# A two-layer decoder trunk on one core: TensorE's part of gates and routing issued later, routing ahead of gates, 95 instead of 78 first products ahead

## The chip, the cores and the metric

The kernel runs on one core of a Trainium2 chip. The metric is the device time of one execution in microseconds (us); lower is better.

## The reference, cut to what matters

512 tokens of width 1024 go through two layers. Each layer has a token mixer and then a product-key expert mixer (`peer`), both with a residual. The change touches the expert mixer alone.

```python
q = (t @ w_q).reshape(n_tok, 8, 2, 64)
scores = jnp.einsum('thpk,hpnk->thpn', q, sub_keys)
s_top, i_top = lax.top_k(scores, 16)
cand = s_top[:, :, 0, :, None] + s_top[:, :, 1, None, :]
...
best, pos = lax.top_k(cand, 16)
expert = jnp.take_along_axis(cand_idx, pos, axis=-1)
gates = jax.nn.softmax(best, axis=-1)
...
u = u_emb[eb]
act = jax.nn.gelu(jnp.einsum('td,thkd->thk', tb, u)) * gb
out = jnp.einsum('thk,thkd->td', act, v_emb[eb])
```

Each token picks 16 of 16384 experts in each of 8 heads, 128 in all. An expert is a row of `u` and a row of `v`.

## The kernel before, in words

The 512 tokens are four tiles of 128. Tile 0 (`GT`) takes its experts by gathers: rows of `u` and `v` come by indirect DMA (`gather`), VectorE multiplies and sums the `u` rows (`products`, tile `junk`), TensorE sums the `v` rows (`sums`, tile `av`), and VectorE adds them to the residual `x`. The gathers run beside the rest, a few at a time (`take`), and `EARLY` says how many are taken before the blocks begin.

Tiles 1 to 3 (`DT`, 384 tokens) go through all 16384 experts as dense products, in 128 blocks of 128 experts. `up(b)` is the first product of block b: 24 matmuls of 384 columns into `pu`, whose activation goes to `H`. The 32-bit weights are split into two bfloat16 halves, so that every product is three matmuls (`mm3`): ScalarE makes `whi` (L71), GpSimd or VectorE `wlo` (L72). `block(b)` multiplies `H` by the gates `G` of that block and makes the second products into six accumulators `acc`.

The gates are dense too: expert by token. They are made in a stage ahead of the blocks, tile by tile. `routing(i)` scores the keys (TensorE, tile `ps`, whose key matrix comes by a DMA on ScalarE's queue), finds the sixteen best on VectorE, and ends with three transposes on TensorE into `pt` (L748 to L750), which ScalarE copies to `i1T`, `i2T` and `ghl`. `gate_group(n)` then serves 16 tokens: VectorE makes four masks (`o2`, `ol`, `oh`, L921 to L926), TensorE multiplies them token by token into `pg`, four tokens in a bank (L932, L933), ScalarE evacuates these into `st` (L934), and a DMA on its queue writes 1 MB to `Gd` in memory (L935). A tile has eight such groups. `oh` and `st` have one buffer each.

Between these steps stand the fillers. The stage is cut into units: one for each step of a routing, three for each gate group, `UNITS` = 183. `fill(n)` counts n units and at each issues its share of the early gathers and of the first products. The products of blocks 0 to `RUN[1]` - 1 = 77 are made so, ahead of the blocks; those of blocks below `SPILL` = 60 are written to `Hd` and read back by `again` two blocks before use, and the other 18 (`AHEAD`) stay in the ring `H`. In the blocks, `block(b)` makes the further first products, one for each block from 60 on, and `tick` takes gathers. A scheduler orders the instructions of each engine by priority within what the data allow, so an engine's order can differ somewhat from the code's.

The order of the stage, before:

```python
            for i in DT:
                for _ in routing(i):
                    fill(1)
                for n in range(NG // ND):
                    gate_group(DT.index(i) * (NG // ND) + n)
                    fill(3)
```

Of the kernel before, what the change touches and what calls it, by code (L numbers as in the profile page):

```python
# [14 lines left out]
F32 = mybir.dt.float32  # L15
BF = mybir.dt.bfloat16
I32 = mybir.dt.int32
U32 = mybir.dt.uint32
AF = mybir.ActivationFunctionType
# [18 lines left out]
DT = [1, 2, 3]  # L38
# [5 lines left out]
KEYS = 128  # L44

KB = 8
GB = 16
NG = TD // GB

SPILL = 60  # L50
AHEAD = 18
LEAD = 6
PACE = 1
OUT1 = 6
RUN = [0] + [min(KEYS, AHEAD + max(b, SPILL)) for b in range(KEYS)]
SLACK = 12
# [1 line left out]
PARTS = 4  # L58

UNITS = ND * 37 + 3 * NG  # L60
EARLY = 80
SHARE = 8
END = 2

# [10 lines left out]
def mm3(nc, out, pairs, start=True, stop=True):  # L75
    n = len(pairs)
    for i, ((ah, al), (bh, bl)) in enumerate(pairs):
        nc.tensor.matmul(out, ah, bh, start=start and i == 0, stop=False)  # L78
        nc.tensor.matmul(out, ah, bl, start=False, stop=False)  # L79
        nc.tensor.matmul(out, al, bh, start=False, stop=stop and i == n - 1)  # L80


class Stream:
# [20 lines left out]
    def next(self, a):  # L104
        while len(self.ready) < self.ahead and self.drams:
            self.emit()
        return tuple(p.rearrange("p (a b) -> p a b", a=a) for p in self.ready.pop(0))
# [420 lines left out]
def layer(tc, nc, k, A, l):  # L528
    ut, vt = A["u"][l], A["v"][l]
    with ExitStack() as es:  # L530
        dram = es.enter_context(tc.tile_pool(name=f"dram{l}", bufs=1, space=bass.MemoryType.DRAM))
        Gd = dram.tile([KEYS // KB, 128, NG, KB * GB], F32, name="Gd")
        Hd = dram.tile([SPILL, 128, TD], F32, name="Hd")
        left = ExitStack()
# [101 lines left out]
        def routing(i):  # L636
# [30 lines left out]
            for a in list(range(8)) + [8]:  # L667
                if a < 8:
                    n = CAND[a]
                    s1, s2 = top[:, :, 0, a:a + 1].to_broadcast([128, HEADS, n]), top[:, :, 1, :n]  # L670
                    i1, i2 = tf[:, :, 0, a:a + 1].to_broadcast([128, HEADS, n]), tf[:, :, 1, :n]
                else:
                    n = 8
# [18 lines left out]
            for a in range(5):  # L692
                n = CAND8[a] if a < 4 else 4
# [7 lines left out]
            for j0, h0, nh in ((0, 0, 4), (0, 4, 4), (8, 0, 2), (8, 2, 2), (8, 4, 2), (8, 6, 2)):  # L701
                n = NCAND if j0 else NC8
# [41 lines left out]
            e2 = rt.tile([128, 2, NS], F32, tag="e2", name="e2", bufs=1)  # L744
            nc.vector.tensor_copy(e2, ei)
            ts = slice(i * 128 - D0, (i + 1) * 128 - D0)
            pt = pr.tile([128, 4, 128], F32, tag="r", name="pt")
            nc.tensor.transpose(pt[:, 0], e2[:, 1], k.ident)  # L748
            nc.tensor.transpose(pt[:, 1], e2[:, 0], k.ident)
# [13 lines left out]
        with ExitStack() as e2:  # L763
# [3 lines left out]
            ahead = pre.enter_context(tc.tile_pool(name=f"ps_a{l}", bufs=2, space=PSUM, reuse_waits="tile"))  # L767
            first = late.enter_context(tc.tile_pool(name=f"first{l}", bufs=2, side="right", reuse_waits="tile"))
# [112 lines left out]
            def take(n):  # L881
                flush()
                for _ in itertools.islice(steps, n):
                    taken[0] += 1
# [9 lines left out]
            def up(b):  # L894
                w = k.W.next(KD)
                p = (psum if b >= RUN[1] or b % 3 == 0 else ahead).tile([128, 512], F32, tag="u", name="pu")[:, :TD]
                mm3(nc, p, [((w[0][:, q], w[1][:, q]), (hhi[:, q], hlo[:, q])) for q in range(KD)])
                if b < SPILL:
                    h = work.tile([128, TD], F32, tag="Hs", name="Hs", bufs=3)
                else:  # L900
                    h = H[b] = work.tile([128, TD], F32, tag="H", name="H", bufs=AHEAD + 1)
                nc.scalar.activation(h, p, AF.Gelu_apprx_tanh)  # L902
                if b < SPILL:
                    nc.scalar.dma_start(Hd[b], h)

            def again(b):
                if b < SPILL:
                    H[b] = work.tile([128, TD], F32, tag="Hs", name="Hs", bufs=3)
                    nc.sync.dma_start(H[b], Hd[b])

            def gate_group(n):

                ts = slice(n * GB, (n + 1) * GB)
                shape = [128, GB // 2, KEYS, 2]

                def by_token(x):
                    return x[:, ts].rearrange("p (a b) -> p a b", b=2)[:, :, None].to_broadcast(shape)

                keys = iot[:, None].to_broadcast(shape)
                o2 = first.tile(shape, BF, tag="o2", name="o2")  # L920
                nc.vector.tensor_tensor(o2, keys, by_token(i2T), op=OP.is_equal)  # L921
                ol = first.tile(shape, BF, tag="ol", name="ol")
                nc.vector.tensor_tensor(ol, keys, by_token(i1T), op=OP.is_equal)
                oh = first.tile(shape, BF, tag="oh", name="oh", bufs=1)
                nc.vector.tensor_tensor(oh, ol, by_token(ghl[:, 0]), op=OP.mult)
                nc.vector.tensor_tensor(ol, ol, by_token(ghl[:, 1]), op=OP.mult)  # L926
                st = first.tile([128, KEYS, GB], F32, tag="st", name="st", bufs=1)
                for c in range(0, GB, 4):
                    pv = ahead.tile([128, 4, KEYS], F32, tag="g", name="pg", bufs=3)
                    for t in range(4):  # L930
                        a, j = divmod(c + t, 2)
                        nc.tensor.matmul(pv[:, t], o2[:, a, :, j], oh[:, a, :, j], start=True, stop=False)  # L932
                        nc.tensor.matmul(pv[:, t], o2[:, a, :, j], ol[:, a, :, j], start=False, stop=True)  # L933
                    nc.scalar.activation(st[:, :, c:c + 4], pv.rearrange("p t k -> p k t"), AF.Copy)  # L934
                nc.scalar.dma_start(Gd[:, :, n].rearrange("p e x -> e p x"),  # L935
                                    st.rearrange("e (p k) t -> e p (k t)", k=KB))

            units, ups = [0], iter(range(RUN[1]))

            def share_of(n):  # L940
                return units[0] * n // UNITS - (units[0] - 1) * n // UNITS

            def fill(n):
                for _ in range(n):
                    units[0] += 1
                    take(share_of(EARLY))
                    for j in itertools.islice(ups, share_of(RUN[1])):
                        up(j)

            for i in DT:  # L950
                for _ in routing(i):
                    fill(1)
                for n in range(NG // ND):
                    gate_group(DT.index(i) * (NG // ND) + n)
                    fill(3)
            for j in ups:
                up(j)
            flush()
# [61 lines left out]
def program(tc, A, out):  # L1020
    nc = tc.nc
    k = Ctx()
    with ExitStack() as es:
        const = es.enter_context(tc.tile_pool(name="const", bufs=1, reuse_waits="tile"))
        k.small = es.enter_context(tc.tile_pool(name="small", bufs=2, reuse_waits="tile"))
        k.W = Stream(nc, es.enter_context(tc.tile_pool(name="wst", bufs=1, reuse_waits="tile")))
        k.ident = const.tile([128, 128], F32, name="ident")
        make_identity(nc, k.ident)
        k.eps = const.tile([128, 1], F32, name="eps")
        nc.vector.memset(k.eps, EPS)  # L1030
        k.junk = const.tile([128, D], BF, name="junk")
        k.x, k.order = [], list(range(NT))
        for i in range(NT):
            x = const.tile([128, D], F32, name=f"x{i}")
            nc.sync.dma_start(x, A["x"][i * 128:(i + 1) * 128, :])
            k.x.append(x)
        for l in range(2):
            layer(tc, nc, k, A, l)
        last = es.enter_context(tc.tile_pool(name="last", bufs=2, side="right", reuse_waits="tile"))
        g = last.tile([128, D], F32, tag="gain", name="gain", bufs=1)  # L1040
        nc.sync.dma_start(g, A["final_norm"].to_broadcast([128, D]))
        for i in k.order:
            h = last.tile([128, D], F32, tag="hrow", name="hrow", bufs=4)
            norm_rows(nc, k, i, g, h)
            nc.sync.dma_start(out[i * 128:(i + 1) * 128, :], h)
# [95 lines left out]
```

## Time and profile before

| what | value |
|---|---|
| median of 3 runs | 3656.72 us (3650.55 to 3668.97) |
| the profiled execution | 3656.95 us, its span 3655.1 us |
| mean granted TensorE clock | 0.961 |
| TensorE busy | 3238.0 us (89%) |
| VectorE, ScalarE, GpSimd busy | 2333.4, 1445.0, 1899.5 us |

The span is the time from the first to the last instruction. Busy time is the time in which at least one instruction of the engine was at work. The page of the profile names groups of instructions by line, engine and tile; the windows give the busy time of each engine in a stretch; the waits say what an idle engine was released by. PE is TensorE, DVE VectorE, ACT ScalarE, POOL GpSimd, and SP the engine whose queue issues most loads.

### The profile page before, as it was taken

To read this page: it belongs to the slowest core of one execution; us is meant where nothing else is said; L and a number is where in the kernel's file an instruction comes from. 1 tells how busy PE (TensorE), PEld (TensorE's weight loads), DVE (VectorE), ACT (ScalarE), POOL (GpSimd) and SP (SyncE) were. 2 spreads that over 40 slices of the span, in tenths; PEclk is the share of its full clock that TensorE was granted. 3 is DMA by queue.
4 is the path that set the end of the run, shared out by engine and by line. 5 is a ranking of instruction groups with operands and counts; after the bars stand their busy time and mean duration, and the time that the engine had idled before them with its cause. 6 is when DMAs were issued, how large, how long until landed. Compare 5 with 4: busy or idle time off the path is not lost. (4 is left out here: it accounts for less than half of the span.)

```text
span 3655.1 us, 52111 instructions
## 1 busy us (share of the span) xinstructions
PE 3238.0 (89%) x19558; PEld 1737.9 (48%) x19786; DVE 2333.4 (64%) x4302; ACT 1445.0 (40%) x2303; POOL 1899.5 (52%) x1106
## 2 busy tenths in 40 slices
PE   8999977877879999999988888778787799999999
PEld 4444554544434444444455555445454344444443
DVE  6554388787756656643567774796868566656534
ACT  5454433333333333333445565333333333333333
POOL 4445755555546566655233345554555356666552
PEclk9999988989989999999999999989998899999999
DMA  4223656877789987886322124568786899878773
GB/s 147 81 89 109 188 171 225 267 225 240 235 306 351 349 300 269 280 292 237 119 77 63 59 71 153 160 216 260 240 268 195 295 345 354 314 283 285 277 264 127
DMA packets 326844, 803.00 MB, mean 220 GB/s; under 512 B 26816, under 2 KB 165568, under 8 KB 322496
## 3 DMA queue, kind: packets, MB, share of 16 engines
q1 hardware_dynamic: 126720, 446.78, 36.6%
q0 software_dynamic: 73728, 268.47, 20.6%
q10 hardware_dynamic: 126144, 84.43, 7.3%
q8 instruction: 155, 2.54, 0.3%
q14 instruction: 97, 0.79, 0.1%
HBM read 723.54 MB, written 76.02 MB: 219 GB/s over the span
## 5 line engine op out<-in xcount | busy, mean ns | idle before, releaser
L72 POOL TENSOR_TENSOR wlo<-w,whi 128x1024 bf16<-128x1024 f32 x520 | 1178.9, 2269 | 1363.7 <-ACT whi L71 1325.8
L71 ACT ACTIVATE whi<-w 128x1024 bf16<-128x1024 f32 x696 | 730.3, 1051 | 769.4 <-PE pu L79 387.5
L78 PE MATMUL pu<-hh,whi 128*128 128x384 bf16 x2048 | 686.1, 335 | 18.2 <-ACT Hs L902 18.2
L79 PE MATMUL pu<-hl,whi 128*128 128x384 bf16 x2048 | 685.2, 335 | 0.0
L80 PE MATMUL pu<-hh,wlo 128*128 128x384 bf16 x2048 | 684.7, 334 | 0.0
L79 PE MATMUL acc<-wlo,ah 128*128 128x512 bf16 x1492 | 567.3, 380 | 34.5 <-ACT ah L71 27.5
L80 PE MATMUL acc<-whi,al 128*128 128x512 bf16 x1492 | 567.2, 380 | 2.3
L78 PE MATMUL acc<-whi,ah 128*128 128x512 bf16 x1470 | 558.9, 380 | 2.3
L807 DVE CUSTOM_DVE_ANT_0 junk<-g,hr 128x1024 bf16<-128x1024 f32 x256 | 360.7, 1409 | 88.2 <-DMA g<-u_in,ix 74.3
L78 PEld LDWEIGHTS <-whi 128*128 128x128 bf16 x2944 | 293.0, 100 | 246.6 <-issue 67.4
L72 DVE TENSOR_TENSOR al<-a,ah 128x384 bf16<-128x384 f32 x256 | 151.5, 592 | 400.8 <-ACT ah L71 400.4
L79 PEld LDWEIGHTS <-whi 128*128 128x128 bf16 x2944 | 293.1, 100 | 217.6 <-issue 40.5
L778 POOL DMA_INDIRECT g<-v_in,ix x256 | 322.3, 1259 | 139.6 <-PE av L832 85.5
L71 ACT ACTIVATE ah<-a 128x384 bf16<-128x384 f32 x256 | 133.6, 522 | 648.5 <-issue 482.3
L80 PEld LDWEIGHTS <-wlo 128*128 128x128 bf16 x2944 | 293.3, 100 | 197.8 <-issue 19.6
L778 POOL DMA_INDIRECT g<-u_in,ix x256 | 307.8, 1202 | 110.6 <-issue 33.7
L72 DVE TENSOR_TENSOR wlo<-w,whi 128x1024 bf16<-128x1024 f32 x176 | 215.0, 1222 | 210.0 <-ACT whi L71 210.0
L78 PEld LDWEIGHTS <-ah 128*128 128x128 bf16 x1536 | 150.4, 98 | 258.6 <-ACT ah L71 54.1
L80 PEld LDWEIGHTS <-al 128*128 128x128 bf16 x1536 | 150.5, 98 | 182.4 <-issue 1.4
L79 PEld LDWEIGHTS <-ah 128*128 128x128 bf16 x1536 | 150.6, 98 | 172.2 <-issue 5.1
L932 PE MATMUL pg<-oh,o 128*128 128x128 bf16 x768 | 108.8, 227 | 111.7 <-ACT st L934 62.8
L79 PE MATMUL mm<-hlo,whi 128*128 128x512 bf16 x500 | 191.1, 382 | 1.4 <-DVE hlo L72 0.5
(384 smaller groups left out, 4942.3 us busy)
## 6 DMA issues: line engine op xcount, KB each, us to landing
w<-ut_in SPq DMA_DIRECT2D x256, 512.0 KB, 4.0
w<-v_in SPq DMA_DIRECT2D x256, 512.0 KB, 5.2
Gd<-st ACTq DMA_DIRECT2D x48, 1024.0 KB, 6.9
G<-Gd SPq DMA_DIRECT2D x32, 1536.0 KB, 8.3
w<-w_in SPq DMA_DIRECT2D x88, 512.0 KB, 3.6
w<-wo_in SPq DMA_DIRECT2D x64, 512.0 KB, 3.7
Hd<-Hs ACTq DMA_DIRECT2D x120, 192.0 KB, 5.3
Hs<-Hd SPq DMA_DIRECT2D x120, 192.0 KB, 6.3
```

What stands on the lines that cost most here:

```text
L71: nc.scalar.activation(hi, src, AF.Copy)
L72: return (lo_eng or nc.vector).tensor_tensor(lo, src, hi, op=OP.subtract)
L78: nc.tensor.matmul(out, ah, bh, start=start and i == 0, stop=False)
L79: nc.tensor.matmul(out, ah, bl, start=False, stop=False)
L80: nc.tensor.matmul(out, al, bh, start=False, stop=stop and i == n - 1)
L778: nc.gpsimd.indirect_dma_start(out=g, out_offset=None, in_=tab, in_offset=bass.IndirectOffsetOnAxis(ap=ix, axis=0))
L807: nc.vector.tensor_tensor_reduce(k.junk, g, hr, op0=OP.mult, op1=OP.add, scale=1.0, scalar=0.0, accum_out=h[:, s:s + 1])
L932: nc.tensor.matmul(pv[:, t], o2[:, a, :, j], oh[:, a, :, j], start=True, stop=False)
```

## The change

The constants change: `SPILL` from 60 to 84, `AHEAD` from 18 to 11, so that `RUN[1]` goes from 78 to 95; `EARLY` from 80 to 100. `routing` yields `True` ahead of its transposes, and `route` puts that last part, and `gate_group` its matmuls, evacuations and write (`multiply`), into a list `due` that `fill` empties three units later. `oh` and `st` get a second buffer. The tiles' routings and gates are issued in the order routing 1, routing 2, gates 1, routing 3, gates 2, gates 3. The shares of the first products are counted for 89 (`REST` = 6 fewer), and what is left is issued after the last group.

```diff
-SPILL = 60
-AHEAD = 18
+SPILL = 84
+AHEAD = 11
...
-EARLY = 80
+EARLY = 100
+
+REST = 6
...
             nc.vector.tensor_copy(e2, ei)
             ts = slice(i * 128 - D0, (i + 1) * 128 - D0)
+            yield True
             pt = pr.tile([128, 4, 128], F32, tag="r", name="pt")
             nc.tensor.transpose(pt[:, 0], e2[:, 1], k.ident)
...
-                oh = first.tile(shape, BF, tag="oh", name="oh", bufs=1)
+                oh = first.tile(shape, BF, tag="oh", name="oh")
                 nc.vector.tensor_tensor(oh, ol, by_token(ghl[:, 0]), op=OP.mult)
                 nc.vector.tensor_tensor(ol, ol, by_token(ghl[:, 1]), op=OP.mult)
-                st = first.tile([128, KEYS, GB], F32, tag="st", name="st", bufs=1)
-                for c in range(0, GB, 4):
...
-                    nc.scalar.activation(st[:, :, c:c + 4], pv.rearrange("p t k -> p k t"), AF.Copy)
-                nc.scalar.dma_start(Gd[:, :, n].rearrange("p e x -> e p x"),
-                                    st.rearrange("e (p k) t -> e p (k t)", k=KB))
-
-            units, ups = [0], iter(range(RUN[1]))
+
+                def multiply():
+                    st = first.tile([128, KEYS, GB], F32, tag="st", name="st")
+                    for c in range(0, GB, 4):
...
+                        nc.scalar.activation(st[:, :, c:c + 4], pv.rearrange("p t k -> p k t"), AF.Copy)
+                    nc.scalar.dma_start(Gd[:, :, n].rearrange("p e x -> e p x"),
+                                        st.rearrange("e (p k) t -> e p (k t)", k=KB))
+
+                due.append((units[0] + 3, multiply))
+
+            units, ups, due = [0], iter(range(RUN[1])), []
...
-                    for j in itertools.islice(ups, share_of(RUN[1])):
+                    for j in itertools.islice(ups, share_of(RUN[1] - REST)):
                         up(j)
-
-            for i in DT:
-                for _ in routing(i):
-                    fill(1)
+                    while due and due[0][0] <= units[0]:
+                        due.pop(0)[1]()
+
+            def route(i):
+                st = routing(i)
+                for last in st:
+                    if last:
+                        due.append((units[0] + 3, lambda: next(st, None)))
+                    else:
+                        fill(1)
+                    if last:
+                        return
+
+            def gate(i):
                 for n in range(NG // ND):
                     gate_group(DT.index(i) * (NG // ND) + n)
                     fill(3)
+
+
+            for i in DT:
+                route(i)
+                if i != DT[0]:
+                    gate(i - 1)
+            gate(DT[-1])
+            while due:
+                due.pop(0)[1]()
             for j in ups:
                 up(j)
             flush()
```

How the instructions move is seen at three places. The line numbers of the changed kernel are two to five higher.

The first is ScalarE at the end of the first routing of layer 0. `sc<-ps` is the evacuation of a head's scores, of the next routing here; `i1T`, `i2T` and `ghl` come from the transposes; `st` is the first gate group. Before, and then with the change:

```order
L71 ACTIVATE whi<-w_5460 128x1024
L902 ACTIVATE Hs<-pu 128x384
L751 ACTIVATE i1T<-pt 128x128
L904 DMA Hd<-Hs 128x384
L752 ACTIVATE i2T<-pt 128x128
L71 ACTIVATE ghl<-pt 128x128
L71 ACTIVATE whi<-w_5546 128x1024
...
L934 ACTIVATE st<-pg 128x128x4 x4
```

```order
L905 ACTIVATE Hs<-pu 128x384
L655 ACTIVATE sc<-ps 128x256
L907 DMA Hd<-Hs 128x384
L651 DMA key<-keys_in 128x256
L73 ACTIVATE whi<-w_5539 128x1024
...
L754 ACTIVATE i1T<-pt 128x128
L755 ACTIVATE i2T<-pt 128x128
L73 ACTIVATE ghl<-pt 128x128
L651 DMA key<-keys_in 128x256
```

The copies of the transposes now come after the first heads of the next routing, and no gate group follows them.

The second is VectorE where the first masks of tile 1 are made (`o`, `ol`, `oh`). Before, they stand behind the end of the same tile's routing; with the change, among the maxima of the next tile's:

```order
L745 CAST e_5312<-ei 128x256
L807 ISA junk,hk<-g,hr 128x1024
...
L921 TENSOR_TENSOR o_5322<-iot,i2T 128x2048
L72 TENSOR_TENSOR ghl<-pt,ghl 128x128
L923 TENSOR_TENSOR ol<-iot,i1T 128x2048
L921 TENSOR_TENSOR o_5408<-iot,i2T 128x2048
L925 TENSOR_TENSOR oh<-ol,ghl 128x2048
```

```order
L661 MATCH_REPLACE sc_5585<-wk,sc 128x128
L663 MAX_INDEX ui<-wk,sc_5579 128x8
L662 MAX wk<-sc_5585 128x8
L924 TENSOR_TENSOR o_6355<-iot,i2T 128x2048
L663 MAX_INDEX ui<-wk,sc_5585 128x8
L926 TENSOR_TENSOR ol<-iot,i1T 128x2048
L659 MAX wk<-sc 128x8 x2
```

The third is ScalarE at the end of the stage; `ah<-a` is the input of the first block. Before, and then with the change:

```order
L902 ACTIVATE H<-pu 128x384
L71 ACTIVATE whi<-w_9461 128x1024
L934 ACTIVATE st<-pg 128x128x4 x4
L935 DMA Gd<-st 128x16x128
L71 ACTIVATE ah<-a_9418 128x384
```

```order
L939 ACTIVATE st<-pg 128x128x4 x4
L940 DMA Gd<-st 128x16x128
L905 ACTIVATE H<-pu 128x384
L73 ACTIVATE whi<-w_9950 128x1024
L73 ACTIVATE whi<-w_9983 128x1024
L905 ACTIVATE H<-pu 128x384
L73 ACTIVATE whi<-w_10016 128x1024
L905 ACTIVATE H<-pu 128x384
L73 ACTIVATE ah<-a_10076 128x384
```

First products and weight splits now stand between the last write of gates and the first block.

## Rows read from the trace of the kernel before

**Rows 1.** The page: the span, and busy us (share) xinstructions of each engine.

```profile
span 3655.1 us, 52111 instructions
...
PE 3238.0 (89%) x19558; PEld 1737.9 (48%) x19786; DVE 2333.4 (64%) x4302; ACT 1445.0 (40%) x2303; POOL 1899.5 (52%) x1106
```

**Rows 2.** Windows by stage; stretch, length, busy us of PE, PEld, DVE, ACT, POOL, clock, DMA.

```profile
517.00:1042.00 525.00, 403.77 (x2775) 240.66 (x2775) 396.23 (x908) 179.47 (x296) 276.14 (x156) 0.90 0.74 239
2369.00:2890.00 521.00, 401.77 (x2765) 239.92 (x2764) 395.05 (x903) 179.16 (x293) 274.45 (x156) 0.91 0.75 240
1042.00:1797.00 755.00, 746.38 (x3876) 345.63 (x3952) 429.94 (x552) 265.98 (x367) 419.82 (x264) 1.00 0.81 288
2890.00:3647.00 757.00, 750.48 (x3898) 347.65 (x3974) 428.60 (x554) 264.98 (x368) 417.69 (x262) 1.00 0.80 284
```

**Rows 3.** Waits of PE, 517 to 1043 us: us in total, times, longest.

```profile
PE pg L932 <- ACT st L934: 29.9, 13, 4.4
PE pg L932 <- DVE oh L925: 26.3, 8, 12.2
PE acc L79 <- ACT ah L71: 13.8, 1, 13.8
PE pt L748 <- DVE e L745: 13.4, 1, 13.4
PE av L832 <- DVE x L836: 10.5, 2, 8.8
PE pu L78 <- ACT Hs L902: 9.6, 2, 6.5
PE ps L651 <- DMA key<-keys_in: 9.6, 4, 5.9
```

**Rows 4.** Waits of ACT and DVE in the same stage.

```profile
ACT st L934 <- DMA Gd<-st: 63.6, 19, 8.4
...
DVE oh L925 <- PE pg L932: 49.1, 15, 6.4
```

**Rows 5.** Windows of the tile pu alone: busy us of PE and of ACT, clock, DMA.

```profile
537.00:568.00 31.00, 30.40 (x186) 2.36 (x5) 1.00 0.77 252
517.00:1042.00 525.00, 332.53 (x1822) 37.17 (x77) 0.90 0.74 239
```

**Rows 6.** Window of the tile av alone in the first layer's blocks: PE, PEld, DVE.

```profile
1042.00:1797.00 755.00, 55.40 (x416) 8.18 (x416) 35.34 (x52) 1.00 0.81 288
```

**Rows 7.** Windows, columns as in rows 2: 50 us of the stage, the first blocks.

```profile
850.00:900.00 50.00, 39.04 (x223) 22.09 (x219) 36.76 (x201) 15.45 (x26) 28.58 (x19) 0.93 0.85 285
1042.00:1300.00 258.00, 254.24 (x1204) 108.68 (x1228) 172.56 (x237) 91.11 (x124) 148.44 (x96) 0.99 0.92 343
```

**Rows 8.** The page's costliest groups, the products of gathered rows: busy us, mean ns.

```profile
L807 DVE CUSTOM_DVE_ANT_0 junk<-g,hr 128x1024 bf16<-128x1024 f32 x256 | 360.7, 1409 | 88.2 <-DMA g<-u_in,ix 74.3
```

**Rows 9.** The page's DMA issues: count, KB each, us to landing.

```profile
w<-ut_in SPq DMA_DIRECT2D x256, 512.0 KB, 4.0
...
Gd<-st ACTq DMA_DIRECT2D x48, 1024.0 KB, 6.9
G<-Gd SPq DMA_DIRECT2D x32, 1536.0 KB, 8.3
```

**Rows 10.** Timeline of PE around the first routing's end: start us, us, what, idle before.

```profile
598.10 0.47 PE L748 MATMUL pt<-ident,e 128*128 128x128 f32 x1 [13.41 <-DVE e L745]
...
598.79 0.53 PE L78 MATMUL pu<-hh,whi 128*128 128x384 bf16 x1
599.11 0.53 PE L79 MATMUL pu<-hl,whi 128*128 128x384 bf16 x1
```

**Rows 11.** Timeline of DVE and of POOL, 568 to 576 us.

```profile
568.34 0.56 DVE L707 TENSOR_TENSOR eq<-cpos,pf 128x800 bf16<-128x800 bf16 x1
...
572.58 2.50 DVE L707 TENSOR_TENSOR eq<-cpos,pf 128x800 bf16<-128x800 bf16 x1
...
572.52 2.12 POOL L72 TENSOR_TENSOR wlo<-w,whi 128x1024 bf16<-128x1024 f32 x1 [7.52 <-ACT whi L71]
```

More of the change, by code (lines that the diff above doesn't have):

```diff
@@ L923, in gate_group @@
                 nc.vector.tensor_tensor(ol, keys, by_token(i1T), op=OP.is_equal)
-                oh = first.tile(shape, BF, tag="oh", name="oh", bufs=1)
+                oh = first.tile(shape, BF, tag="oh", name="oh")
                 nc.vector.tensor_tensor(oh, ol, by_token(ghl[:, 0]), op=OP.mult)
                 nc.vector.tensor_tensor(ol, ol, by_token(ghl[:, 1]), op=OP.mult)
-                st = first.tile([128, KEYS, GB], F32, tag="st", name="st", bufs=1)
-                for c in range(0, GB, 4):
[L929 to L933, printed above, removed]
-                    nc.scalar.activation(st[:, :, c:c + 4], pv.rearrange("p t k -> p k t"), AF.Copy)
-                nc.scalar.dma_start(Gd[:, :, n].rearrange("p e x -> e p x"),
-                                    st.rearrange("e (p k) t -> e p (k t)", k=KB))
-            units, ups = [0], iter(range(RUN[1]))
+                def multiply():
+                    st = first.tile([128, KEYS, GB], F32, tag="st", name="st")
+                    for c in range(0, GB, 4):
+                        pv = ahead.tile([128, 4, KEYS], F32, tag="g", name="pg", bufs=3)
+                        for t in range(4):
+                            a, j = divmod(c + t, 2)
+                            nc.tensor.matmul(pv[:, t], o2[:, a, :, j], oh[:, a, :, j], start=True, stop=False)
+                            nc.tensor.matmul(pv[:, t], o2[:, a, :, j], ol[:, a, :, j], start=False, stop=True)
+                        nc.scalar.activation(st[:, :, c:c + 4], pv.rearrange("p t k -> p k t"), AF.Copy)
[3 more added lines that the diff above has]
+            units, ups, due = [0], iter(range(RUN[1])), []
             def share_of(n):
```

## The prediction, made before the changed kernel was run

> **What bounds the kernel now.** I read the page first for the share of each engine, then the windows by stage, then the waits of the slow stage, then single stretches of the timeline. One execution spans 3655.1 us and TensorE is busy for 3238.0 of them [rows 1]; no other engine comes near. The windows then show two kinds of stage, each found once per layer [rows 2]. The blocks (757 us and 755 us) are TensorE from end to end: 746.4 of 755 us busy at a granted clock of 1.00. There a product that is taken away shortens the run by its own length. The stage ahead of them, which routes three token tiles and makes their gates, takes 525 and 521 us, and TensorE works for 403.8 of 525 at a mean clock of 0.90. It is idle for 121 us while VectorE is busy for 396.2, the DMA for 0.74 of the time, and nobody is full. So this stage is bound by engines that wait for each other in turn, and it has room for work if those waits can be filled.
>
> The waits of TensorE name the turns [rows 3]: 29.9 us for ScalarE to empty a bank of gates (st), 26.3 for VectorE's masks (oh), 13.8 for the first block's input, 13.4 for the end of a routing (pt), 10.5 for a residual sum, 9.6 for an evacuation, 9.6 for a key's load. Behind the first of these stands a DMA: ScalarE waits 63.6 us for the write of the only st buffer, and whatever else it should split or evacuate waits in line. VectorE in turn waits 49.1 us for TensorE to give back the only oh [rows 4].
>
> **The change part by part, for one layer.**
>
> *17 first products move (78 to 95).* In 537 to 568 us 186 matmuls of first products take 30.40 us at full clock, 163 ns each [rows 5]; a product has 24, so 3.92 us, and 17 have 66.7 us. In the blocks this is saved whole, because TensorE idles for 9 of 755 us there [rows 2]. EARLY also takes 20 gathers ahead. The order of instructions shows 60 instead of 48 second-product matmuls (av) ahead of the first block, three halves of four; 416 records in the blocks are 52 halves for 55.40 us [rows 6], 1.07 us each, 3.2 us in all. Blocks: **-70 us**. The gating stage has the same 70 us of TensorE work more.
>
> What else these products issue: each has a weight load of 512 KB, a ScalarE split and evacuation, and a GpSimd split. 24 more of them (SPILL 60 to 84) are written to memory and read back in the blocks, on the queues of ScalarE and SP. I cost the blocks' reads at nothing. The first blocks already run with such reads at a DMA share of 0.92, and TensorE is busy for 254.2 of 258 us beside it [rows 7]; the change makes that stretch longer (84 blocks instead of 60), not denser, because by the code's counts the gathers per tick stay the same: some 181 over 166 ticks, now some 160 over 149. The 258 us hold the first sixty-odd blocks, so 84 are about 350 us; if the cover went, each per cent by which the transfers fell behind would cost 3.5 us a layer.
>
> *The stage's waits.* The end of a routing (pt) is issued three units later, with the next tile's routing ahead of it. Units carry 0.49 products each (89 over 183, 0.43 before), so about 1.5 products, 6 us, are put ahead of the wait, and three more come from the denser filling. VectorE needs some 6 us more up to there itself (three products at 1.41 [rows 8], and stretched operations, below). I keep 6 of 13.4. For the masks the order shows the first two groups of a tile made inside the next tile's routing, and oh has a second buffer: I keep 5 of 26.3. With two st buffers ScalarE no longer stands still for the write. What is left for TensorE is a split of some 1 us in front of an evacuation: I keep 11 of 29.9. With more products queued TensorE gets to the evacuations later, while VectorE's part of the routing is as long: 3 of 9.6. Before the first block stand four products after the last gates, 15.7 us, against a write of 6.9 and a read of 8.3 us [rows 9] and the block's own first operations. That would cover nearly all of it, but the SP queue now has only two second weights ahead of the three gate reads, where it had seven. The third block's weight queues behind 4.5 MB of gates, so I keep 7 of 13.8. This is what is late next. The residual sum (10.5) and the key loads (9.6) are not touched, and of the remaining 8 us I keep 5. The 121 us become 57: **-64 us**.
>
> *The clock.* [...] In the whole stage 1822 records of first products take 332.53 us instead of 298 (1822 by 163 ns) [rows 5]; a part of these 35 us is only the ends of interrupted runs. [...]
>
> *VectorE and GpSimd.* GpSimd splits 17 more weights, and a compare beside such a split takes 2.50 us instead of 0.56 [rows 11]: 1.9 us for each that is hit, between nothing and 33 us. Nine products more come to 13 us. VectorE then works 409 to 442 us, under the 515 forecast, so I add nothing. ScalarE (179 us of 525) and GpSimd (276) have room for their part [rows 2].
>
> *The sum.* Stage: 525 + 70 - 64 - 16 = 515. Blocks: 755 - 70 = 685. A layer gives back 80 us, and the two are alike within 4 us in all four windows [rows 2], so 160 us. The profiled execution took 3656.95 us, 1.9 more than its span and 0.2 more than the median of the three runs, so no correction is made: **3497 us**.
>
> **The rivals.**
>
> *A: transfers set the stage.* It moved 525 us at 239 GB/s, 125.5 MB [rows 2]. The change adds 17 weights, 20 gathers of the same size and 24 products of 0.2 MB, 24.1 MB, together 149.6. The densest 50 us that I found in the stage reach 285 GB/s [rows 7]; at that rate the stage needs 525 us and gives nothing, 140 us remain: 3517 us. For it: the masks' writes, 1 MB a group, are now bunched behind the last routing. Against it: the blocks hold 343 GB/s [rows 7], by which the stage needs 436. Chance 0.20.
>
> *B: the waits only change place.* VectorE is at work for 396 of 525 us [rows 2], and if its own order sets the stage, TensorE's 70 us come on top: saved and spent cancel, 3657 us, no change. Against it: 49 us of VectorE's idling are waits for the oh that is now doubled [rows 4]. Chance 0.04.
>
> *C: slower, through the clock.* [...] Chance 0.03. [...]
>
> *D: better.* [...] Chance 0.08.
>
> That the change does not do what it says is excluded by the order of instructions: 95 products stand ahead of the first block.
>
> **How the numbers follow.** The forecast has 0.65. Its own spread comes from what I kept of the waits: 30 us of waits and 10 lost to the clock give -111 us a layer (3435), 78 and 22 give -51 (3555). 3435 to 3555 takes in A as well and leaves out B, C and D, 0.15 together, and a little of the forecast's own edges. About half a per cent, 18 us, is what a measurement of this kernel can tell from no change: faster by more is forecast, A and D, 0.93; the same is B, 0.04; slower is C, 0.03.
>
> **What would show it.** In the profile after: blocks of about 685 us at clock 1.00 with TensorE still idle for some 1%; a stage of 500 to 530 us with TensorE about 89% busy (458 of 515) and a clock of about 0.95; no wait of st for the write of Gd and none of oh for TensorE; four products between the last gates and the first block. The forecast is wrong if the blocks show new waits for weights or read-back products, if the stage grows by more than 20 us, or if TensorE waits at pt and st as long as now. A stage near 525 us with a DMA share above 0.9 would be A.

## The result and the profile after

The changed kernel takes 3533.28 us (median of 4 runs, 3529.10 to 3548.67), the kernel before 3653.64 beside it: a ratio of 0.9673, 95% interval 0.963 to 0.9715. The forecast was 3497 us and a gain of 160; 120 came.

The page and the windows by stage of the changed kernel; the columns are those of [rows 2]. As there, the first layer's window of the blocks ends at the first of their residual sums; the table further below runs to the last one and has some 6 us more.

```profile
span 3527.3 us, 52345 instructions
...
PE 3201.8 (91%) x19574; PEld 1728.5 (49%) x19786; DVE 2307.3 (65%) x4286; ACT 1444.2 (41%) x2303; POOL 1931.2 (55%) x1122
```

```profile
515.00:1044.40 529.40, 454.67 (x3186) 275.48 (x3185) 436.55 (x914) 201.40 (x326) 348.21 (x189) 0.93 0.84 280
2299.00:2833.20 534.20, 455.21 (x3190) 275.64 (x3188) 431.25 (x918) 201.37 (x326) 347.71 (x190) 0.93 0.83 278
1044.40:1726.30 681.90, 675.23 (x3457) 305.12 (x3523) 375.42 (x522) 242.97 (x333) 361.79 (x237) 1.00 0.83 298
2833.20:3520.50 687.30, 680.57 (x3479) 307.23 (x3544) 379.57 (x526) 242.24 (x335) 358.57 (x235) 1.00 0.82 293
```

Against [rows 2] the blocks fell from 755 and 757 us to 682 and 687, with TensorE still idle for 1% of them. The gating stage, forecast to fall from 525 to 515, grew to 529 and 534. The waits of TensorE in it, against [rows 3]:

```profile
PE av L835 <- DVE x L839: 29.3, 7, 15.5
PE pu L80 <- ACT Hs L905: 23.8, 2, 13.8
PE pg L938 <- DVE ol L929: 5.7, 5, 1.9
PE ps L653 <- DVE ghl L74: 4.6, 1, 4.6
PE pg L937 <- DVE oh L928: 3.9, 1, 3.9
PE pg L937 <- ACT st L939: 3.7, 7, 2.5
...
PE pt L751 <- DVE e L747: 0.4, 1, 0.4
```

The four waits at which the change aims have nearly gone: st 29.9 to 3.7, oh 26.3 to 3.9, pt 13.4 to 0.4, the first block 13.8 to none. Two others took over: the residual sum 10.5 to 29.3, the evacuation of a first product 9.6 to 23.8. The first comes from VectorE directly. The second comes from it through ScalarE, whose timeline (start, us, what, idle before) shows it standing 17.16 us for a subtraction on VectorE before it goes on to the split and the evacuation:

```profile
580.46 0.31 ACT L720 ACTIVATE wk<-wk 128x128 f32<-128x128 f32 x1 [17.16 <-DVE wk L719]
...
580.91 1.06 ACT L73 ACTIVATE whi<-w 128x1024 bf16<-128x1024 f32 x1
581.99 1.28 ACT L905 ACT_TABLE_LOAD   x1
583.28 0.49 ACT L905 ACTIVATE Hs<-pu 128x384 f32<-128x384 f32 x1
```

The longest wait for a residual sum, 15.54 us, has another side. `av` has one buffer, so TensorE cannot make the next half before VectorE has added the last one to `x`. Below stand the half made before, the sum that it waits for, and the half made after it:

```profile
833.50 1.06 PE L835 MATMUL av<-g,z 128*32 128x512 f32 x8
850.29 0.68 DVE L839 TENSOR_TENSOR x<-x,av 128x512 f32<-128x512 f32 x1
851.03 1.94 PE L835 MATMUL av<-g,z 128*32 128x512 f32 x8 [15.54 <-DVE x L839]
```

In between VectorE worked through the compares of a routing's end. So not only how much VectorE has to do may set such a wait, but also behind what the sum stands in its order. No run here changes that order, or the number of `av` buffers, alone.

The windows of single stretches (columns as before) show how VectorE's load lies: the second routing and the last gates.

```profile
600.00:702.00 102.00, 84.84 (x488) 48.25 (x486) 100.17 (x295) 32.70 (x53) 72.76 (x41) 0.90 0.75 253
...
960.00:1044.00 84.00, 78.36 (x649) 50.83 (x647) 57.65 (x41) 38.36 (x65) 54.65 (x27) 1.00 0.99 342
```

In the second routing VectorE is busy for 100.2 of 102 us; in the last gates for 57.7 of 84, while the DMA stands at 0.99; but TensorE is busy there for 78.4 of 84 us, so at most 5.6 us of the stage are lost in that stretch. Three causes were open for the stage: VectorE (V below), ScalarE's standing (H), or the transfers (D).

### The profile page after: what moved, and what is told of

It is laid out like the page before. It is cut to its first block, busy times and chain, and to the rows that moved or that the text cites. A ratio compares the mean times of both kernels' runs of the same rounds, so it can differ in the third digit from the quotient of the medians.

```text
span 3527.3 us, 52345 instructions
## 1 busy us (share of the span) xinstructions
PE 3201.8 (91%) x19574; PEld 1728.5 (49%) x19786; DVE 2307.3 (65%) x4286; ACT 1444.2 (41%) x2303; POOL 1931.2 (55%) x1122
## 5 line engine op out<-in xcount | busy, mean ns | idle before, releaser
L74 POOL TENSOR_TENSOR wlo<-w,whi 128x1024 bf16<-128x1024 f32 x536 | 1201.9, 2244 | 1223.1 <-ACT whi L73 1136.9
L81 PE MATMUL pu<-hl,whi 128*128 128x384 bf16 x2048 | 677.9, 331 | 0.0
L82 PE MATMUL pu<-hh,wlo 128*128 128x384 bf16 x2048 | 677.2, 331 | 0.2
L810 DVE CUSTOM_DVE_ANT_0 junk<-g,hr 128x1024 bf16<-128x1024 f32 x256 | 382.0, 1492 | 100.7 <-DMA g<-u_in,ix 93.6
L781 POOL DMA_INDIRECT g<-u_in,ix x256 | 321.7, 1257 | 106.3 <-issue 34.5
L74 DVE TENSOR_TENSOR wlo<-w,whi 128x1024 bf16<-128x1024 f32 x160 | 196.3, 1227 | 19.6 <-ACT whi L73 19.2
L835 PE MATMUL av<-g,z 128*32 128x512 f32 x1024 | 141.6, 626 | 65.4 <-DVE x L839 65.4
L1008 DVE TENSOR_TENSOR a<-Hs,G 128x384 f32<-128x384 f32 x168 | 159.2, 948 | 58.6 <-DMA G<-Gd 47.0
```

The lines of the kernel that those rows point to most:

```text
L74: return (lo_eng or nc.vector).tensor_tensor(lo, src, hi, op=OP.subtract)
L781: nc.gpsimd.indirect_dma_start(out=g, out_offset=None, in_=tab, in_offset=bass.IndirectOffsetOnAxis(ap=ix, axis=0))
L810: nc.vector.tensor_tensor_reduce(k.junk, g, hr, op0=OP.mult, op1=OP.add, scale=1.0, scalar=0.0, accum_out=h[:, s:s + 1])
L835: m = nc.tensor.matmul(av[32 * j:32 * j + 32, :], z[:, j, a * 32:a * 32 + 32], rows[j][:, c * 512:(c + 1) * 512], start=True, stop=True)
L1008: nc.vector.tensor_tensor(a.rearrange("p (a b) -> p a b", b=GB), H[b].rearrange("p (a b) -> p a b", b=GB), g, op=OP.mult)
```

## The experiments

The table gives for each run its first products and early gathers ahead of the blocks, the stage (from 15 us after tile 0's indices are made to the first second product) and the blocks (from there to the last residual sum), each for layer 0 and layer 1 of the profiled execution, the median and, with its interval, the ratio to the kernel before as it ran beside each (medians of 3653.64 to 3658.74 us).

| run | products, EARLY | stage, us | blocks, us | run, us | ratio |
|---|---|---|---|---|---|
| before | 78, 80 | 525, 521 | 761, 758 | 3653.64 | 1 |
| the change | 95, 100 | 530, 535 | 688, 687 | 3533.28 | 0.9673 (0.963 to 0.9715) |
| e1_order_only | 78, 80 | 465, 466 | 761, 760 | 3548.17 | 0.9718 (0.9685 to 0.9751) |
| e2_count_only | 95, 100 | 588, 593 | 683, 682 | 3647.07 | 0.9987 (0.9966 to 1.0009) |
| e3_early80 | 95, 80 | 507, 503 | 702, 700 | 3505.81 | 0.9605 (0.9572 to 0.9637) |
| e4_exp_early | 95, 100 | 534, 522 | 688, 690 | 3529.27 | 0.9663 (0.9631 to 0.9696) |
| e5_half_products | 95, 100 | 504, 503 | 689, 688 | 3472.41 | 0.9496 (0.948 to 0.9511) |
| e6_half_rows | 95, 100 | 500, 505 | 690, 687 | 3474.82 | 0.9511 (0.9495 to 0.9527) |
| e7_tile_order | 95, 100 | 541, 539 | 689, 689 | 3557.28 | 0.9736 (0.9719 to 0.9752) |
| e8_one_st | 95, 100 | 574, 578 | 689, 691 | 3621.57 | 0.9902 (0.9886 to 0.9919) |
| e9_early60 | 95, 60 | 473, 475 | 725, 730 | 3486.13 | 0.9524 (0.9495 to 0.9552) |
| e10_rows_in_gates | 95, 80 | 523, 519 | 704, 701 | 3544.23 | 0.9687 (0.9658 to 0.9717) |
| e11_even_transfers | 95, 72 | 499, 491 | 699, 698 | 3482.15 | 0.9529 (0.9515 to 0.9543) |

### e1_order_only and e2_count_only: the two halves of the change

```diff
# e1, against the change
-SPILL = 84
+SPILL = 67
-EARLY = 100
+EARLY = 80
# e2, against the kernel before
-SPILL = 60
-AHEAD = 18
-EARLY = 80
+SPILL = 84
+AHEAD = 11
+EARLY = 100
```

e1 has 78 products as before, of which 67 instead of 60 are written to memory.

> The change with 78 first products and 80 early gathers as before (SPILL 67, AHEAD 11, EARLY 80): the order and the second buffers alone. Three theories of where the 15 to 20 us a layer went that the changed stage took beyond the forecast. V: in a routing VectorE's own queue is full, and TensorE is held at the places where it needs VectorE. H: ScalarE's in-order queue, standing for an exponential or a gelu that VectorE is not ready for, holds TensorE; VectorE itself has room. D: transfers, late gathers above all. By the forecast's own sum (waits and clock give 80 us a layer, whatever is added) the stage is 445 us and the run 3497. V and D: the routings stay VectorE's length, 485 to 500 us a stage, 3585 to 3610. H: 470 us, 3550.

> The kernel before with SPILL 84, AHEAD 11, EARLY 100 alone: 95 products in the old order with single buffers of oh and st. If the added products fill nothing of the waits (rival B of the prediction), the stage is 595 us and the run 3655. If they fill the waits at a routing's end and at the masks, where VectorE is late, the stage is 560 to 570 and the run 3600 (V and H alike). D: the denser transfers add to it, 580 us or more, 3625.

First row: the window of the first layer's stage in e1; second: the same in e2, with the two longest waits of TensorE in it.

```profile
515.00:979.80 464.80, 388.62 (x2742) 239.51 (x2740) 396.72 (x893) 179.02 (x291) 272.91 (x150) 0.92 0.81 266
```

```profile
518.00:1106.00 588.00, 475.04 (x3222) 281.16 (x3221) 421.71 (x928) 203.73 (x328) 339.36 (x193) 0.91 0.77 255
...
PE pg L932 <- ACT st L934: 31.3, 13, 5.4
PE av L832 <- DVE x L836: 25.2, 5, 12.2
```

The order and the buffers alone take 60 and 55 us from the stage and carry 106 us of the run. That lies between the forecast's own sum (445 us) and what V and D gave (485 to 500), nearest to H's 470. VectorE has the same work there as in the kernel before (396.7 against 396.2 us). The count alone takes 78 and 76 us from the blocks and puts 63 and 72 on the stage: the run does not change. That is the outcome of rival B, in the old order; B's mechanism, VectorE's own order, is not shown by it, as the longest wait is still the one for the only st buffer. Together the two give only 15 us more than the order alone: most of what the added work saves in the blocks is spent in the stage.

### e3_early80: the early gathers alone

```diff
-EARLY = 100
+EARLY = 80
```

> The change with EARLY 80 instead of 100: some 12 products of gathered rows fewer for VectorE in the stage and 10 MB fewer to transfer, the same 95 first products. V: VectorE's routings shorten by 12 to 18 us a layer, the blocks lengthen by 3 to 6, run 3510. D: the stage shortens by 25 to 35 us a layer, run 3480. H: the stage within 5 us, run 3535 to 3540.

```profile
521.00:1028.30 507.30, 447.45 (x3156) 276.39 (x3154) 422.78 (x895) 201.38 (x325) 317.83 (x171) 0.94 0.81 271
1028.30:1730.80 702.50, 687.80 (x3519) 308.73 (x3584) 405.67 (x550) 249.83 (x343) 388.06 (x258) 1.00 0.84 306
```

The stage is 22 and 32 us shorter than with 100, the blocks 14 and 12 us longer, the run 3505.81 us. Against e1 the 17 products now cost the stage 42 and 37 us and save 59 and 60 in the blocks. So the products pay, and the 20 gathers do not. H had the stage within 5 us, and that does not hold. V's figure lies near in the run and D's in the stage, so the cause needed a run that parts VectorE's work from the transfers.

### e5_half_products and e6_half_rows: VectorE's work or the transfers

```diff
# e5, against the change
-nc.vector.tensor_tensor_reduce(k.junk, g, hr, op0=OP.mult, ...)
+nc.vector.tensor_tensor_reduce(k.junk[:, :512], g[:, :512], hr[:, :512], op0=OP.mult, ...)
# e6, added to e5, for u
+row, src = (g[:, :512], tab.rearrange("e (h x) -> (e h) x", h=2)) if tab is ut else (g, tab)
-nc.gpsimd.indirect_dma_start(out=g, out_offset=None, in_=tab, ...)
+nc.gpsimd.indirect_dma_start(out=row, out_offset=None, in_=src, ...)
```

> The change, with VectorE's product of a gathered u row taken over 512 of 1024 columns (the other half of each dot product is left out); the transfers are as in the change. e3 showed that the 20 more early gathers cost 22 to 32 us of stage a layer; this asks whether as VectorE's work (V) or as transfers (D). V: VectorE has some 35 us a stage less to do, the stage falls by 20 to 30 us a layer, run 3475 to 3490. D: the stage within 5 us, run 3520 to 3535.

> As e5_half_products, and the u rows are gathered as half rows too (512 columns from a table seen as twice as many half rows, so other values; the same number of gathers). Against e5: some 16 MB less to transfer in a stage. V: within 5 us a layer of e5. D: 20 to 30 us of stage a layer below e5, run 3475 if e5 stays at 3530.

The product of a gathered row in the stage (ns least, median, most), in the change and in e5, with the stage of e5 and TensorE's waits for residual sums in it, and the stage of e6:

```profile
L810 DVE CUSTOM_DVE_ANT_0 junk<-g,hr x64: 1198/1220/3768, 528.3 to 971.9; 128x1024 bf16<-128x1024 f32 x64
```

```profile
L810 DVE CUSTOM_DVE_ANT_0 junk<-g,hr x64: 662/688/2761, 529.5 to 950.3; 128x512 bf16<-128x512 f32 x64
...
515.50:1019.90 504.40, 451.99 (x3201) 275.46 (x3199) 397.47 (x929) 202.04 (x326) 332.26 (x191) 0.95 0.86 293
...
PE av L835 <- DVE x L839: 23.8, 4, 15.6
```

```profile
515.00:1015.50 500.50, 451.24 (x3179) 274.59 (x3177) 388.81 (x914) 200.32 (x325) 324.95 (x189) 0.95 0.80 260
```

VectorE has 39 us less to do (436.6 to 397.5), with the transfers as they were, even denser at 293 GB/s. The stage falls by 25 and 32 us and the run by 61, a little more than V gave. Taking half of the `u` rows' bytes away as well (260 GB/s) changes nothing: 3474.82 against 3472.41, the intervals overlap. So VectorE's work is part of what sets the stage, and the bytes of the `u` rows are not. VectorE was busy for 82% of the stage and yet each us taken from it gave back some 0.6 to 0.9 us.

VectorE's busy time is not the whole cause. The longest wait for a residual sum stays at 15.6 us with the products halved. And in e3 VectorE had only 14 us less to do (436.6 to 422.8), for nearly the same gain in the stage: what else 20 gathers bring, such as residual sums, issues on GpSimd and bytes of `v` rows, costs as well, and no run parts these.

### e4_exp_early: ScalarE's standing

```diff
             nc.vector.tensor_copy(pf, pos)
+            nc.vector.tensor_tensor(gt, best, ..., op=OP.subtract)
+            nc.scalar.activation(gt, gt, AF.Exp)
...
-            nc.vector.tensor_tensor(gt, best, ..., op=OP.subtract)
-            nc.scalar.activation(gt, gt, AF.Exp)
```

> The change with the routing's subtraction and exponential moved ahead of its twelve compare steps, so that ScalarE need not stand for them. H: the wait of TensorE for ScalarE's evacuation (23.8 us a stage) falls by at least 14 and the stage by 12 to 18, run 3500. V: ScalarE's stand goes, but TensorE then waits as long at the next place that needs VectorE (masks, residual sum), stage within 5 us, run 3525 to 3535. D as V.

```profile
PE av L835 <- DVE x L839: 27.9, 6, 17.3
PE pu L80 <- ACT Hs L905: 14.6, 2, 8.5
PE pt L751 <- DVE e L747: 12.3, 1, 12.3
```

ScalarE's standing for the subtraction, in the change and in e4:

```profile
ACT wk L720 <- DVE wk L719: 22.5, 3, 17.2
...
ACT wk L692 <- DVE wk L691: 28.7, 3, 12.9
```

The edit did not do what was wanted: ScalarE stands for the subtraction at its new place too, for 28.7 instead of 22.5 us in all. TensorE's wait through ScalarE fell from 23.8 to 14.6, less than the 14 us that H asked for, and 12.3 us appeared at the end of the routing, which needs VectorE. The first layer's stage grew by 4 us, the second's fell by 13, and the run is the change's within the interval. So H has no support here, but e4 does not rule it out; what speaks against it is e3.

### e7_tile_order and e8_one_st: which part of the order

```diff
# e7
             for i in DT:
                 route(i)
-                if i != DT[0]:
-                    gate(i - 1)
-            gate(DT[-1])
+                while due:
+                    due.pop(0)[1]()
+                gate(i)
# e8
-st = first.tile([128, KEYS, GB], F32, tag="st", name="st")
+st = first.tile([128, KEYS, GB], F32, tag="st", name="st", bufs=1)
```

> The change with the old order of tiles: routing 1, gates 1, routing 2, and so on, each routing's end issued at once; the gates' multiplication stays deferred, the second buffers stay. If the routing put ahead is what removes the waits at pt and at the masks, they come back (13 and some 20 us) and the stage is 555 to 565, run 3590 to 3600. If the deferral and the buffers did it, the stage is within 10 us, run 3535 to 3550.

> The change with one buffer of st again: ScalarE must wait for each write of gates before it evacuates the next group. If that wait carried its 30 us of TensorE's waiting, the stage grows by 20 to 30 us, run 3575 to 3590. If transfers set the gates' pace (D), ScalarE's wait falls into time that is lost anyway: 5 to 10 us a layer, run 3545. V: 20 us, since VectorE has room in the gates and TensorE does not.

Waits of TensorE in the first layer's stage, in e7 and in e8:

```profile
PE pg L937 <- DVE oh L928: 13.2, 3, 6.9
PE pg L938 <- DVE ol L929: 11.4, 9, 2.9
PE ps L653 <- DMA key<-keys_in: 11.3, 3, 9.2
PE pt L751 <- DVE e L747: 8.0, 1, 8.0
```

```profile
PE pg L937 <- ACT st L939: 53.9, 17, 8.3
...
ACT st L939 <- DMA Gd<-st: 61.3, 12, 9.0
```

In the old order of tiles the waits at masks and pt stand at 33 us instead of 10 and the key loads at 11.3 instead of 0.9, but the residual sum and the evacuations give back part (22.7 and 13.8 instead of 29.3 and 23.8), and the stage is 11 and 4 us longer, near the second case. So the routing put ahead, with its deferred end, is worth some 8 us of stage a layer; the run is 24 us longer, of which the stages hold 15. The second buffer of st is worth 44 and 43 us, well above the 20 to 30 that I gave it: with one, TensorE waits 53.9 us for ScalarE, which waits 61.3 us for the write. The second buffer of oh was not run alone.

### e9, e10, e11: how many early gathers, and where

```diff
# e9
-EARLY = 100
+EARLY = 60
# e10: take() at a unit of a routing 0.30 rows, at one of the gates 0.64 (80 in all)
-EARLY = 100
+EARLY = 30, 64
...
-                    take(share_of(EARLY))
+                    rows[0] += EARLY[n > 1]
+                    take(rows[0] // 100 - (rows[0] - EARLY[n > 1]) // 100)
# e11
-EARLY = 100
+EARLY = 72
+LATE = 135
...
-            ticks = KEYS + KEYS - RUN[1] - SLACK
+            ticks = 100 * SPILL + LATE * (KEYS + KEYS - RUN[1] - SLACK - SPILL)
...
-                pace[0] += 1
+                pace[0] += 100 if b < SPILL else LATE
```

> The change with EARLY 60: 40 early gathers fewer than in the change. V: VectorE has some 30 us a stage less than in the change, the stage is 485 to 495 us (e3, with 80: 505). The blocks pay: 201 gathers on 149 ticks, 1.35 a tick instead of 1.08, which in the 84 first blocks is 0.14 MB more on 1.45 MB a block, where e3 already moves 354 GB/s: blocks 705 to 720 us (e3: 701). Run 3490 to 3515. D would have the stage fall by another 25 us as well, so this run does not tell V from D; it asks where EARLY is best.

> The change with 80 early gathers as in e3, but taken unevenly: 0.30 of one at each unit of a routing, 0.64 at each unit of the gates, so that some 15 of them move from the routings to the gates. V, with the routing as the place where VectorE is full: the routings shorten by some 10 us a layer and the gates have room for it, stage 490 to 497 us, run 3480 to 3495. If it is VectorE's total over the stage that counts, as e3: stage 505, run 3506. D: the gates, which transfer most, become longer: stage 510 to 520, run 3515 to 3530.

> A version meant to beat both: the change with EARLY 72, and in the blocks 1.35 times as many gathers a tick from block 84 on as before it. e9's first 350 us of blocks move 355 GB/s and TensorE is idle for 17.6 us there, its later blocks 274 GB/s with 4.2 of 368 idle. V and the transfers' limit in the blocks together: stage between e9 (473) and e3 (505), 485 to 495 us; the gathers left over, 189, taken so that both parts of the blocks move about 350 GB/s, blocks 690 to 698 us; run 3450 to 3475. If the later blocks do not bear 1.5 gathers a tick, TensorE waits there and the blocks are 705 or more, run 3480 to 3495.

Stage and blocks of the first layer in e9, and the first 350 us of its blocks with the longest wait of TensorE and VectorE's wait for read-back products in them; then the first part of the blocks in the change, with VectorE's wait there, and in e3; then the two parts of e11's blocks:

```profile
517.00:990.00 473.00, 436.98 (x3104) 272.51 (x3102) 400.30 (x865) 200.21 (x325) 293.07 (x150) 0.97 0.83 269
990.00:1715.10 725.10, 703.11 (x3636) 309.51 (x3632) 433.07 (x578) 249.87 (x343) 421.42 (x279) 0.99 0.85 311
...
990.00:1340.00 350.00, 332.43 (x1604) 137.31 (x1601) 244.60 (x323) 117.54 (x158) 213.54 (x143) 0.99 0.95 355
PE av L835 <- DVE x L839: 12.5, 5, 5.0
DVE a L1008 <- DMA Hs<-Hd: 26.8, 11, 4.7
```

```profile
1044.40:1400.00 355.60, 351.57 (x1701) 149.13 (x1733) 244.03 (x329) 127.51 (x173) 210.66 (x134) 1.00 0.93 347
DVE a L1008 <- DMA Hs<-Hd: 4.1, 3, 2.4
...
1028.30:1380.00 351.70, 340.24 (x1639) 143.11 (x1669) 245.09 (x324) 122.82 (x166) 211.55 (x138) 1.00 0.95 355
```

```profile
1013.00:1363.00 350.00, 342.70 (x1645) 146.06 (x1677) 245.61 (x321) 125.08 (x170) 204.83 (x130) 1.00 0.94 354
1363.00:1707.00 344.00, 340.73 (x1873) 159.63 (x1907) 172.83 (x235) 119.50 (x166) 196.38 (x135) 1.00 0.79 280
```

With 60 the stage falls by another 34 and 29 us, below what I gave, and the blocks grow by 23 and 30: in their first part, at 355 GB/s, TensorE is now idle for 17.6 of 350 us, where the change had 4.0 of 355.6 at 347 GB/s. TensorE's own wait there is again for VectorE's residual sums, 12.5 us. VectorE is busy as long as in the change (244.6 and 244.0 us) but stands 26.8 instead of 4.1 us for read-back products. So late transfers are the likely cause, through VectorE; no run takes bytes away from the blocks to show it. In the stage, VectorE's 400 us of work are near e5's 397, and yet e9's stage is 31 and 28 us shorter: the 40 gathers cost beyond VectorE's busy time. The gain of 20 gathers fewer is 28 us at first and 20 after that.

e10 was a miss, outside all three figures: with the same 80 gathers, some of them moved from the routings to the gates, the run is 38 us slower than e3. VectorE has the same work in both (423.3 and 422.8 us). TensorE then waits longer for residual sums, and VectorE for rows; first e3, then e10:

```profile
PE av L835 <- DVE x L839: 13.0, 3, 12.0
DVE junk L810 <- DMA g<-u_in,ix: 31.0, 13, 9.2
```

```profile
PE av L835 <- DVE x L839: 32.3, 5, 10.5
...
DVE junk L810 <- DMA g<-u_in,ix: 43.8, 9, 20.4
```

The evacuations give back most of that (7.1 us instead of 26.0), so of the first layer's 16 us more of stage only 8 are idle time of TensorE, and 8 are busy time. VectorE's lag is then not a matter of the routings alone, as V had it, nor of its total work. What sets these waits, when the same rows come later, is not settled here; where the residual sums fall in VectorE's order is a candidate that was not tested.

e11 has its stage at 499 and 491 us, a little above and within what was expected, and its blocks at 699 and 698, at the upper edge; the run of 3482.15 us misses the 3475 expected at most, and is as good as e9 and no better than it. Both beat the change by some 50 us.

## Why the prediction was right or wrong

The direction and the range held: 3533 lies in 3435 to 3555. The gain was 120 us instead of 160.

*The blocks, -70 a layer:* measured -73 and -70 by the windows. The size was right, its parts were not: e3 against e1 gives 59 us for the 17 products instead of 66.7. TensorE's busy time in the blocks fell by 64 us (751.8 to 687.8), and its idle time rose by 5; that the same gathers then fall on fewer blocks is the likely reason, not a tested one. The change against e3 gives 14 and 12 us for the 20 gathers, where I had counted 3.2. The added read-back products brought no wait of TensorE in the change, as forecast.

*The waits, -64:* measured 121 to 75 us, -46; in the full sum this is the term that was mis-sized. The four at which the change aims went further than I had it: 13.7 us left with the masks' second row, instead of 29. The key loads, kept at 9.6, fell to 0.9. The two that I left alone or let fall grew: the residual sum (kept at 10.5) to 29.3, the evacuations (kept at 3) to 23.8.

*The clock, -16:* the stage's mean granted clock went from 0.90 to 0.93, not to the 0.95 forecast. No run shows the 16 us as a term, nor the 10 and 22 us of the range: they come from an estimate of mine, 30 us lost to the clock before and 14 after. What the runs show in its place is TensorE's busy time, which rose by 51 us (403.8 to 454.7) for 70 us of added work by the forecast's count, so the rest of it became some 19 us shorter; no run parts what the clock has in that.

*VectorE, "so I add nothing":* this is the step that failed, and it stands behind the two waits that grew. Its size was right (409 to 442 us, measured 436.6), and I set it against the length of the stage, 515, as if an engine below 100% cost nothing. e5 shows what it costs: 39 us fewer on VectorE shorten the stage by 25 and 32 us. The 20 early gathers, which the prediction charged with 3.2 us of TensorE and with 13 us of VectorE that it then set at nothing, put 22 to 32 us on the stage (e3). How much of that is VectorE's work, and how much the place of its residual sums or the gathers' other work, stays open.

*That the range held is in part luck.* Taken apart by the runs, the three parts of the stage's sum were each off, and the errors nearly cancel. The order and the buffers gave 60 and 55 us (e1), not 80, with no work added to VectorE. The 17 products then cost 42 and 37 us (e3 against e1), not 70. The 20 gathers cost 22 and 32, not nothing. That makes 530 and 535 us instead of 515.

*Rival A* named a time, 3517, nearer to the result than the forecast, but not the mechanism: e6 takes 33 GB/s of the 293 away against e5 and nothing changes, and the stage's DMA share of 0.84 stays under the 0.9 that was to be A's sign. *Rival B* had the outcome of the count alone (e2) and not of the whole. *Rival C*, slower through the clock, did not come: the run is 120 us shorter, and the stage's clock rose from 0.90 to 0.93. *Rival D*, a gain above the forecast's, did not come either; e9 has a stage of 473 and 475 us, with 40 gathers fewer, and pays for it in the blocks (725 and 730 us instead of 688 and 687).

## What to carry to other kernels

An engine under 100% busy is not free when others wait for it. Here VectorE was busy for 82% of the stage, TensorE waited 53 of its 75 idle us for it, directly or through ScalarE, and 39 us of work taken from it gave back 25 and 32. So put a price on work that such an engine gets, and look for the waits that name it. The busy time alone does not give that price: with about 400 us of VectorE's work the stage was 504 us in e5 and 473 in e9. Where a change raises several counts at once, run each count alone; here one of them (17 products) paid and another (20 gathers) took part of it back. The second buffer on a write to memory, one word in the code, carried more than the new order of tiles.

## What the runs showed of the hardware

Not expected was how little the transfer rate tells of what it costs. The first blocks bear 347 GB/s at a DMA share of 0.93 with TensorE 4.0 us idle in 355.6 (the change). At 355 GB/s and 0.95 it is idle for 11.5 us in 351.7 in e3 and for 17.6 in 350 in e9, while VectorE's wait for read-back products in e9 is 26.8 us against 4.1 in the change. In the stage a share of 0.86 at 293 GB/s (e5) cost nothing that could be measured against 0.80 and 260 (e6).
